# Two transformer blocks with mixtures of experts: the second passes of a pair under one branch behind the down products, the overflow loop moved into the last pair's first unit

## The chip, the cores and the metric

The kernel runs on one core of one Trainium2 chip. The metric is the device time of one execution in microseconds, the median of several runs. Engines: TensorE (PE; PEld is its weight load), VectorE (DVE), ScalarE (ACT), GpSimd (POOL) and SyncE (SP, which issues most loads). A q behind a name (PEq, DVEq, PEldq) is the engine's sequencer, which issues instructions, takes branches and waits on semaphores.

## The reference

Two blocks follow each other on 256 tokens of width 1024: retention and convolution with a mixture of 32 experts, then gMLP and windowed attention with a mixture of 16 experts. Each token goes to two experts. The first mixture, cut to what matters:

```python
eid = grp_idx * EXPERTS_PER_GROUP + top_i
combine = jnp.einsum('nk,nke->ne', top_w, jax.nn.one_hot(eid, N_EXPERTS, dtype=jnp.float32))
y = jnp.zeros(t.shape, jnp.float32)
for e in range(N_EXPERTS):
    h = jax.nn.silu(t @ p['w_exp_gate'][e]) * (t @ p['w_exp_up'][e])
    y = y + combine[:, e:e + 1] * (h @ p['w_exp_down'][e])
```

The second mixture is of the same form with 16 experts. The tokens of one expert are a matter of the data, so the kernel reads counts at run time and branches on them.

## The kernel before

Both mixtures run through `run` (L835). Experts go in pairs: a pair's tokens stand in 64 slots each, gathered by one-hot matmuls into X. Iteration p of the loop does, in this order: the gate and up products of pair p (`unit`, L637, on 32 slots of each expert; `up_more` does the other 32 under a branch, L870, if the expert has more than 32 tokens), with `turn` called between the two halves of the first unit's matmuls; the down products of pair p - 1 (`down`, L676); the gather of pair p + 1 (`gather`, L522, in two PSUM banks); the scatter of pair p - 1 into the sums (`scatter`, L705). Iteration p = n/2 has only the last down products and their scatter. `turn` transposes the hidden rows eh and the one-hots of the pair before (L656, L664) for `down`.

`down` makes two halves o of the output columns, 8 matmul rows each in the built program, with a call `between(o)` in each half after 4 rows. After each half ScalarE makes yh (L679) and VectorE yl (L680).

The first mixture takes at most 64 tokens of an expert this way and the second up to 96: there, `second_up` (branch L787, taken if expert e has more than 64 tokens) does gate and up for 32 more, and `second_down` (L799 for the pair, L802 for each expert) its down products and scatter, two iterations later. Anything beyond goes to `overflow` (L713 to L765; its branch is L719), a loop over a list, one item at a time, which is empty with these data. A count is a register that TensorE, VectorE and ScalarE each load (`count`, L777) before the branch. An engine that skips a body runs a semaphore instruction in its place, so that the counts of the others come out right. With these data only the first expert of pairs 1 and 5 has more than 64 tokens.

Around the change, before: `again(1)`, called in the second half of `down`, holds the second pass of the pair's first expert (`self.second_up(p, 0, ...)`), and the second pass of the other expert stands behind `down`. At the end of iteration np_ - 1 (p = 15 in the first mixture, p = 7 in the second) stands `overflow`. At p = np_ `turn` runs the second downs of the last two pairs under one branch, L854. Experts' weights are loaded by `prefetch` in a fixed order into a ring of slots; the waits of SyncE for a free slot set when a load starts. `x1.work` and `x2.work` name the slot that the overflow loop uses as its scratch.

Of the kernel before, what the change touches and what calls it, by code (L numbers as in the profile page):

```python
# [10 lines left out]
F32 = mybir.dt.float32  # L11
# [46 lines left out]
def block_kernel(ctx: ExitStack, tc: tile.TileContext, a, out, dbg=None):  # L58
# [326 lines left out]
    class Experts:  # L385
# [449 lines left out]
        def run(self, hooks, twice=False):  # L835
            np_ = self.n // 2
# [9 lines left out]
            for p in range(np_ + 1):  # L846
                p1 = p - 1
                ws = prs[p1][2] if p else None

                def turn():  # L850
                    if p == np_ and twice:
                        for e in range(2 * p - 4, 2 * p):
                            self.w(e, 2)
                        with tc.If(self.count(self.n + np_) > 64):  # L854
                            for q in (p - 2, p1):
                                self.second_down(q, more.pop(q))
                    elif p > 1 and twice:
                        self.second_down(p - 2, more.pop(p - 2))
                    if p:
                        hT = turned.pop(1) if 1 in turned else self.turn_h(st.pop(p1))  # L860
                        turned[0] = hT, self.turn_slots(prs[p1][0])
# [11 lines left out]
                def again(o):  # L873
                    if p == np_:
                        return
                    if o == 0:
                        up_more(1)
                    elif twice:
                        more[p] = self.tile("h2", [128, 512], F32, 2)
                        self.second_up(p, 0, more[p], self.gu_bank)  # L880

# [23 lines left out]
                if twice and p < np_:  # L905
                    self.second_up(p, 1, more[p], self.gu_bank)
                if p + 1 < np_:
                    prs[p + 1] = self.pair(p + 1)
                if p:
                    self.scatter(turned[0][1], ys, last=(p1 == np_ - 1))  # L910
                if p == np_ - 1:
                    self.overflow()
                    if not twice:
                        turned[1] = self.turn_h(st.pop(p))
                if p in hooks:
# [735 lines left out]
    x1.slots = [x0, xb, s4, q0, q1, s3, q2, s2, s0, s1]  # L1651
    x1.work = xb
    ident_b = const.tile([128, 128], BF, name="ident_b", tag="colA")
# [399 lines left out]
    x2.slots = x2.slots + [slot_of(ring) for _ in range(3)] + [slot_of(r_) for r_ in ring2]  # L2053
    x2.work = x2.slots[0]
    other = {"PT": "wr32", "P3": "wr16"}
# [74 lines left out]
```

## Time and profile before

| what | value |
|---|---|
| median of 3 runs | 1430.4 us (1430.01 to 1430.69) |
| profiled execution, its own time | 1430.14 us |
| its span in the profile | 1428.3 us |
| granted TensorE clock, mean | 0.967 |
| TensorE busy | 1301.6 us, 91% of the span |
| VectorE, ScalarE, GpSimd busy | 55%, 37%, 19% |
| first mixture | about 548 to 982 us |
| second mixture | about 1165 to 1419 us |

The busy shares are means over stages. In the first mixture the loads of weights run at 427 GB/s in most slices; in the second one the share of the DMA queues is lower in places and TensorE is 88 to 99% busy. The two blocks' other stages are outside the change. The rows below use these names: ms and gu are PSUM banks, w a slot of weights, P one-hots, hb the token rows, rs a row scale, L line numbers of the kernel before.

### The profile page before, as it was taken

What the parts mean: (1) busy time and instruction counts of PE and PEld (TensorE: products, weight loads), DVE (VectorE), ACT (ScalarE), POOL (GpSimd) and SP (SyncE); (2) the same over time, 40 slices, a digit from 0 to 9 for tenths busy, and PEclk for the clock granted to TensorE, in tenths of its full rate; (3) what the DMA queues carried; (4) which work ended last, traced back from release to release, by engine and by line L of the source; (5) the groups of instructions that cost most, each with busy time, mean ns of one, the idle gap of its engine ahead of it and who ended that gap; (6) DMA issues with size and microseconds to landing.
All of it is one profiled execution on the core that took longest, in us unless ns stands there. A gap on an engine that the chain in (4) does not pass through costs nothing. (4 is left out here: it accounts for less than half of the span.)

```text
span 1428.3 us, 25110 instructions
## 1 busy us (share of the span) xinstructions
PE 1301.6 (91%) x10033; PEld 919.4 (64%) x10033; DVE 791.8 (55%) x1555; ACT 528.9 (37%) x889; POOL 273.6 (19%) x308
## 2 busy tenths in 40 slices
PE   7999999999999889978988889998999999889885
PEld 5898999999999784423433334435999964433432
DVE  2898898988965974422423543235664642234222
ACT  1673747455445423221222112224574432222222
POOL 3023424232334310000201300002340410000000
PEclk9999999999999999999999989999999999999998
DMA  9943363554369576999999999997357375999791
GB/s 330 310 158 119 135 227 126 177 185 172 129 185 350 221 293 285 426 427 429 425 429 427 427 427 428 426 398 263 119 223 303 132 293 240 424 415 423 314 404 68
DMA packets 92857, 417.51 MB, mean 292 GB/s; under 512 B 6464, under 2 KB 26832, under 8 KB 75552
## 3 DMA queue, kind: packets, MB, share of 16 engines
q1 hardware_dynamic: 89600, 409.59, 72.5%
q0 software_dynamic: 3104, 5.80, 1.4%
q8 instruction: 106, 1.74, 0.5%
q14 instruction: 47, 0.39, 0.1%
HBM read 414.29 MB, written 1.08 MB: 291 GB/s over the span
## 5 line engine op out<-in xcount | busy, mean ns | idle before, releaser
L676 PE MATMUL ms<-w,hT 128*64 128x512 f32 x768 | 208.4, 643 | 50.8 <-DMA w<-w_exp_down_dram 40.4
L100 DVE TENSOR_TENSOR wlo<-w,whi 128x1024 fp32r<-128x1024 f32 x151 | 196.2, 1301 | 63.5 <-ACT whi L100 63.3
L100 ACT CAST whi<-w 128x1024 fp32r<-128x1024 f32 x158 | 164.8, 1048 | 145.1 <-PE pj L109 139.2
L676 PEld LDWEIGHTS ms<-w,hT 128*64 128x64 f32 x768 | 61.8, 145 | 193.5 <-issue 135.7
L109 PE MATMUL pj<-uh,whi 128*128 128x256 f32 x512 | 148.2, 289 | 0.0
L109 PE MATMUL pj<-ul,whi 128*128 128x256 f32 x512 | 145.8, 285 | 0.9 <-DVE ul L100 0.7
L109 PE MATMUL pj<-uh,wlo 128*128 128x256 f32 x512 | 145.6, 284 | 0.8 <-DVE wlo L100 0.8
L1165 DVE SCALAR_TENSOR_TENSOR cacc<-zT,dwT,cacc 128x256 f32<-128x256 f32 x240 | 141.9, 591 | 3.3
L637 PE MATMUL gu<-w,X 128*32 128x512 f32 x1184 | 140.9, 597 | 1.7 <-DMA w<-w_exp_up_dram 1.4
L645 POOL MEMSET eh<- 32x512 f32 x47 | 24.4, 518 | 545.7 <-DVEq L870 339.9
L109 PEld LDWEIGHTS pj<-uh,whi 128*128 128x128 f32 x512 | 98.7, 193 | 5.0 <-ACT gt L1348 3.4
L109 PEld LDWEIGHTS pj<-ul,whi 128*128 128x128 f32 x512 | 98.7, 193 | 2.0 <-DVE ul L100 1.7
L109 PEld LDWEIGHTS pj<-uh,wlo 128*128 128x128 f32 x512 | 98.7, 193 | 1.0 <-DVE wlo L100 1.0
L637 PE MATMUL gu<-w,h 128*32 128x512 f32 x768 | 92.4, 615 | 2.1 <-DVE eh L643 1.2
L637 PEld LDWEIGHTS gu<-w,X 128*32 128x32 f32 x1184 | 34.0, 109 | 74.6 <-issue 65.8
L657 DVE COPY hT<-ms 128x512 f32<-128x512 f32 x24 | 16.6, 690 | 95.9 <-PE ms L656 95.9
L683 DVE SCALAR_TENSOR_TENSOR yt<-ms,ws,gt 128x512 f32<-128x512 f32 x32 | 24.0, 750 | 81.3 <-PE ms L676 80.1
L100 ACT CAST yh<-yt 128x512 fp32r<-128x512 f32 x32 | 19.8, 620 | 130.6 <-DVE yt L683 130.6
L109 PE MATMUL pj<-hnh,whi 128*128 128x256 f32 x200 | 56.7, 284 | 0.0
L637 PEld LDWEIGHTS gu<-w,h 128*32 128x32 f32 x768 | 24.2, 112 | 50.4 <-issue 45.2
L109 PE MATMUL pj<-hnl,whi 128*128 128x256 f32 x200 | 56.3, 281 | 0.1
L109 PE MATMUL pj<-hnh,wlo 128*128 128x256 f32 x200 | 55.8, 279 | 0.0
(578 smaller groups left out, 2990.6 us busy)
## 6 DMA issues: line engine op xcount, KB each, us to landing
w<-w_exp_gate_dram SPq DMA_DIRECT2D x31, 2048.0 KB, 23.3
w<-w_exp_up_dram SPq DMA_DIRECT2D x31, 2048.0 KB, 26.1
w<-w_exp_down_dram SPq DMA_DIRECT2D x28, 2048.0 KB, 22.3
w<-w_in_dram SPq DMA_DIRECT2D x19, 2048.0 KB, 8.8
w<-expert_w_gate_dram SPq DMA_DIRECT2D x16, 2048.0 KB, 16.5
w<-expert_w_up_dram SPq DMA_DIRECT2D x16, 2048.0 KB, 20.7
w<-w_ada_dram SPq DMA_DIRECT2D x12, 2048.0 KB, 9.4
w<-expert_w_down_dram SPq DMA_DIRECT2D x12, 2048.0 KB, 12.9
```

Of the source, the lines that this page charges most:

```text
L100: return S.copy(hi, src), eng.tensor_sub(lo, src, hi.bitcast(F32))
L109: PE.matmul(out_ap, l(k), r(k), start=(first and i == 0), stop=(last and i == n - 1))
L637: PE.matmul(gu[o:o + 32], x_of(hf * 4 + j), w_of(i, hf * 4 + j), start=(j == 0), stop=(j == 3), tile_position=(0, o))
L645: zero.memset(h[u0 + 32:u0 + 64], 0.0)
L657: V.tensor_copy(hT, p_)
L676: PE.matmul(dn[o][b * 64:b * 64 + 64], hT[:, c, b * 64:b * 64 + 64], w_of(b, c, o), start=(c == 0), stop=(c == 3))
L683: V.scalar_tensor_tensor(y, dn[o], wc, self.gate[:, o * 512:o * 512 + 512], op0=ALU.mult, op1=ALU.mult)
L1165: i = V.scalar_tensor_tensor(cacc[:, j], zT[:, j, w:w + 256], dwT[:, w, j:j + 1], cacc[:, j], op0=ALU.mult, op1=ALU.add)
```

## The change

Both second passes of a pair go under one outer branch (L907 in the changed file), taken if either expert of the pair has more than 64 tokens, behind all of `down`; the inner branches L787 stay inside it. The second down of pair 5 moves from `turn` of p = 7 to the end of p = 6. `overflow` moves from the end of p = np_ - 1 into its `turn`, behind a `prefetch` of all weights. In the first mixture the last pair's hidden rows are transposed ahead of its predecessor's scatter. The overflow scratch becomes another tile in each mixture. Lines behind L851 shift by 3: L854 is L857, L870 is L873.

```diff
--- before.py
+++ after.py
@@ -848,13 +848,16 @@
                 ws = prs[p1][2] if p else None
 
                 def turn():
+                    if p == np_ - 1:
+                        self.prefetch(3 * self.n)
+                        self.overflow()
                     if p == np_ and twice:
                         for e in range(2 * p - 4, 2 * p):
                             self.w(e, 2)
                         with tc.If(self.count(self.n + np_) > 64):
                             for q in (p - 2, p1):
                                 self.second_down(q, more.pop(q))
-                    elif p > 1 and twice:
+                    elif 1 < p < np_ - 1 and twice:
                         self.second_down(p - 2, more.pop(p - 2))
                     if p:
                         hT = turned.pop(1) if 1 in turned else self.turn_h(st.pop(p1))
@@ -875,9 +878,6 @@
                         return
                     if o == 0:
                         up_more(1)
-                    elif twice:
-                        more[p] = self.tile("h2", [128, 512], F32, 2)
-                        self.second_up(p, 0, more[p], self.gu_bank)
 
                 if p < np_:
                     st[p] = self.tile("eh", [128, 512])
@@ -903,15 +903,18 @@
                     again(0)
                     again(1)
                 if twice and p < np_:
-                    self.second_up(p, 1, more[p], self.gu_bank)
+                    more[p] = self.tile("h2", [128, 512], F32, 2)
+                    with tc.If(self.count(self.n + p) > 64):
+                        for b in range(2):
+                            self.second_up(p, b, more[p], self.gu_bank)
                 if p + 1 < np_:
                     prs[p + 1] = self.pair(p + 1)
+                if p == np_ - 1 and not twice:
+                    turned[1] = self.turn_h(st.pop(p))
                 if p:
                     self.scatter(turned[0][1], ys, last=(p1 == np_ - 1))
-                if p == np_ - 1:
-                    self.overflow()
-                    if not twice:
-                        turned[1] = self.turn_h(st.pop(p))
+                if p == np_ - 2 and twice:
+                    self.second_down(p1, more.pop(p1))
                 if p in hooks:
                     hooks[p]()
 
@@ -1649,7 +1652,7 @@
     s0, s1, s2, s3, s4 = [slot_of(r_) for r_ in ring2]
     q0, q1, q2 = [slot_of(ring) for _ in range(3)]
     x1.slots = [x0, xb, s4, q0, q1, s3, q2, s2, s0, s1]
-    x1.work = xb
+    x1.work = lambda: fin["ra"].rearrange("p a n -> p (a n)")
     ident_b = const.tile([128, 128], BF, name="ident_b", tag="colA")
     G.tensor_copy(ident_b, ident)
     halves = h1.bitcast(BF).rearrange("p t (d two) -> p t d two", two=2)
@@ -2051,7 +2054,7 @@
     psp = es.enter_context(pool("pse", 1, space=PSUM))
     x2 = hp["x2"]
     x2.slots = x2.slots + [slot_of(ring) for _ in range(3)] + [slot_of(r_) for r_ in ring2]
-    x2.work = x2.slots[0]
+    x2.work = x2.slots[8]
     other = {"PT": "wr32", "P3": "wr16"}
 
     def tile_of(name, shape, dt=F32, bufs=1):
```

TensorE, from the down products of p = 3 in the second mixture to the gather of pair 4. L676 is down, L777 a count's load, L522 the matmuls of a gather (128x32: those of a second pass, 128x128: those of the next pair). Before:

```order
L676 MATMUL ms<-w,hT 64x512 x8
L777 TENSOR_LOAD over
L787 COMPARE_AND_BRANCH
...
L787 UNCONDITIONAL_BRANCH x2
L676 MATMUL ms<-w,hT 64x512 x4
L777 TENSOR_LOAD over
L787 COMPARE_AND_BRANCH
...
L787 UNCONDITIONAL_BRANCH x2
...
L522 MATMUL ms<-P,hb_11305 128x128
```
Now:

```order
L676 MATMUL ms<-w,hT 64x512 x12
L777 TENSOR_LOAD over
L907 COMPARE_AND_BRANCH
...
L787 COMPARE_AND_BRANCH
...
L787 COMPARE_AND_BRANCH
...
L787 UNCONDITIONAL_BRANCH x2
L907 UNCONDITIONAL_BRANCH
...
L522 MATMUL ms<-P,hb_11305 128x128
```
The branch between 8 and 4 rows of down products is gone; all stand ahead of the branch L907, and both bodies lie in its reach.

VectorE at the same place. L680 makes yl, L538 the one-hots of a second pass, L526 scales the gathered rows. Before:

```order
L680 SCALAR_TENSOR_TENSOR yl<-ms,ws,yh 128x512
L777 TENSOR_LOAD over
L787 COMPARE_AND_BRANCH
L538 TENSOR_TENSOR P_13962<-slot,pos_12367 128x32 x2
...
L787 UNCONDITIONAL_BRANCH x2
L777 TENSOR_LOAD over
L787 COMPARE_AND_BRANCH
...
L787 UNCONDITIONAL_BRANCH x2
L680 SCALAR_TENSOR_TENSOR yl<-ms,ws,yh 128x512
L526 TENSOR_TENSOR h_12373<-ms,cols 128x512
```
Now:

```order
L680 SCALAR_TENSOR_TENSOR yl<-ms,ws,yh 128x512 x2
L777 TENSOR_LOAD over
L907 COMPARE_AND_BRANCH
L777 TENSOR_LOAD over
L787 COMPARE_AND_BRANCH
...
L787 UNCONDITIONAL_BRANCH x2
L777 TENSOR_LOAD over
L787 COMPARE_AND_BRANCH
...
L907 UNCONDITIONAL_BRANCH
L526 TENSOR_TENSOR h_12373<-ms,cols 128x512
```
Both rows of L680 now stand ahead of the branch and of the gather's release; before, the second stood behind both bodies.

TensorE, from the scatter of p = 7 to the last transposes. L705 is the scatter, L718 the load of the overflow count, L656 the transposes of eh. Before:

```order
L705 MATMUL acc_12299<-yl,PT 128x512
L718 TENSOR_LOAD idi
L719 COMPARE_AND_BRANCH
...
L719 UNCONDITIONAL_BRANCH
L777 TENSOR_LOAD over
L854 COMPARE_AND_BRANCH
L777 TENSOR_LOAD over
L799 COMPARE_AND_BRANCH
...
L854 UNCONDITIONAL_BRANCH
L656 MATMUL ms<-ident,eh 128x128 x4
```
Now:

```order
L705 MATMUL acc_12299<-yl,PT 128x512
L777 TENSOR_LOAD over
L857 COMPARE_AND_BRANCH
L777 TENSOR_LOAD over
L799 COMPARE_AND_BRANCH
...
L857 UNCONDITIONAL_BRANCH
L656 MATMUL ms<-ident,eh 128x128 x4
```
The overflow branch is gone from there. It stands in p = 7's first unit now, between two halves of the matmuls of L637 (w are the unit's weights):

```order
L799 UNCONDITIONAL_BRANCH
L637 MATMUL gu<-w,h_12373 32x512 x8
L718 TENSOR_LOAD idi
L719 COMPARE_AND_BRANCH
...
L719 UNCONDITIONAL_BRANCH
L656 MATMUL ms<-ident,eh 128x128 x4
...
L664 MATMUL ms<-ident_b,P 128x128
L637 MATMUL gu<-w,h_12373 32x512 x8
```
Before, the second down of pair 5 stood there in its place; it has moved ahead, to the end of p = 6.

## Rows read from the trace of the kernel before

**Rows 1.** Waits of TensorE, 1160 to 1428 us: total us, times, longest us.
```profile
PE ms L522 <- DVEq L787: 8.8, 3, 4.8
PE ms L656 <- PEq L854: 4.5, 1, 4.5
PE gu L522 <- issue: 4.3, 2, 2.6
PE ms L522 <- PEq L787: 2.6, 1, 2.6
PE ms L656 <- PEq L799: 1.9, 3, 0.7
```

**Rows 2.** Line L787: duration ns min/median/max, first and last start.
```profile
L787 PEldq COMPARE_BRANCH  x18: 70/338/4207, 1176.2 to 1398.0; - x18
```

**Rows 3.** Line L719, the overflow branch, TensorE's sequencer (PEldq) and SyncE's.
```profile
L719 SPq EVENT_SEMAPHORE  x18: 17/17/17, 960.2 to 1394.9; - x18
...
L719 PEldq COMPARE_BRANCH  x2: 428/786/1145, 969.6 to 1401.5; - x2
```

**Rows 4.** Line L854, the branch over the last two second downs.
```profile
L854 PEldq COMPARE_BRANCH  x1: 2457/2457/2457, 1403.3 to 1403.3; - x1
```

**Rows 5.** Timeline of TensorE, p = 2, 3, 4, 6: start, us, what, [idle before <-releaser].
```profile
1238.61 1.94 PE L676 MATMUL ms<-w,hT 128*64 128x512 f32 x8 [1.30 <-PEq L787]
...
1244.19 1.53 PE L522 MATMUL gu<-P,hb 128*128 128x128 bf16 x22 [1.70 <-issue]
...
1273.98 1.68 PE L522 MATMUL ms<-P,hb 128*128 128x128 bf16 x24
...
1279.49 0.41 PE L522 MATMUL gu<-P,hb 128*128 128x128 bf16 x4 [2.60 <-issue]
...
1302.98 1.65 PE L522 MATMUL ms<-P,hb 128*128 128x128 bf16 x24
...
1371.68 1.68 PE L522 MATMUL ms<-P,hb 128*128 128x128 bf16 x24 [2.60 <-PEq L787]
```

**Rows 6.** Timeline of ScalarE, p = 3, the end of the down products.
```profile
1273.87 0.69 ACT L679 ACTIVATE yh<-ms,ws 128x512 fp32r<-128x512 f32 x1 [2.90 <-PE ms L676]
```

**Rows 7.** Timeline of VectorE, p = 3, the same place.
```profile
1274.59 0.75 DVE L680 SCALAR_TENSOR_TENSOR yl<-ms,ws,yh 128x512 fp32r<-128x512 f32 x1 [2.76 <-ACT yh L679]
```

**Rows 8.** Timeline of TensorE, p = 1, with a second pass that runs.
```profile
1203.01 3.06 PE L522 MATMUL gu<-P,hb 128*128 128x32 bf16 x48 [0.54 <-DVE P L538]
...
1206.67 5.34 PE L637 MATMUL gu<-w,h 128*32 128x512 f32 x32 [0.47 <-DVE rs L584]
...
1215.73 1.75 PE L522 MATMUL ms<-P,hb 128*128 128x128 bf16 x24 [1.85 <-DVEq L787]
1217.28 2.76 PE L522 MATMUL gu<-P,hb 128*128 128x128 bf16 x24
```

**Rows 9.** Timeline of VectorE, p = 1.
```profile
1202.69 0.28 DVE L538 TENSOR_TENSOR P<-slot,pos 128x32 bf16<-128x32 f32 x2
...
1214.86 0.47 DVE L793 TENSOR_SCALAR h<-h,rs 32x512 f32<-32x512 f32 x1
```

**Rows 10.** Windows: busy us (x instructions) of PE, PEld, DVE, ACT, POOL; PEclk, DMA share, GB/s.
```profile
1217.20:1220.70 3.50, 3.50 (x32) 3.40 (x31) 0.85 (x2) 0.62 (x3) 0.00 (x0) 0.51 1.03 435
1235.00:1241.00 6.00, 4.55 (x25) 1.56 (x22) 0.75 (x1) 1.11 (x2) 0.00 (x0) 1.00 0.99 415
1406.30:1411.00 4.70, 4.04 (x14) 2.00 (x16) 0.69 (x1) 0.37 (x1) 0.00 (x0) 0.50 0.03 7
```

**Rows 11.** Timeline of TensorE, the last down products.
```profile
1406.34 1.10 PE L656 MATMUL ms<-ident,eh 128*128 128x128 f32 x4 [4.54 <-PEq L854]
...
1408.27 8.83 PE L676 MATMUL ms<-w,hT 128*64 128x512 f32 x32 [0.62 <-ACT PT L665]
```

**Rows 12.** Timeline of TensorE, the last down products of the first mixture.
```profile
971.85 7.09 PE L676 MATMUL ms<-w,hT 128*64 128x512 f32 x32 [0.72 <-ACT PT L665]
```

**Rows 13.** Timeline of GpSimd, the last memset of the second mixture.
```profile
1394.19 0.52 POOL L645 MEMSET eh<- 32x512 f32 x1 [3.02 <-DVEq L870]
```

## Prediction

> **What bounds the kernel now.** I read the waits of TensorE over the second mixture of experts first (iterations p = 0 to 7 and the last down products, from 1160 us on). TensorE waits there for branches and for instructions, never for a weight load: no row of this list names a DMA [rows 1]. In the names, PEq, DVEq and ACTq are an engine's sequencer; "PEq L787" is TensorE's own branch around a second pass, "DVEq L787" VectorE's. "issue" behind the gather L522 is a wait that the profile gives no cause for. So a microsecond taken off these waits comes off the time, and a new one is added to it.
>
> Next, the branch itself [rows 2]. TensorE's jump over a second pass takes 70 to 4207 ns, median 338. The spread tells what it is: a short jump when the code behind it is at hand, and a fetch when it is not. It costs time only if it outlasts the matmuls already queued. The overflow jump takes TensorE 428 and 1145 ns [rows 3], the one over the two last second downs 2457 ns [rows 4].
>
> The timeline shows where it is paid [rows 5]. Second passes run only for the first expert of p = 1 and p = 5; six iterations skip. In p = 2 the first jump, inside the down products, holds TensorE 1.30 us, and the gather behind the second jump stands still 1.70 us in its middle. In p = 3 the stop in the gather is 2.60 us. In p = 4 nothing is paid: the gather starts at once (1302.98). In p = 6 the second jump holds it 2.60 us. Beside these, the start of each gather lies 0.15 us behind the last down product, which is no term.
>
> **The change part by part** (us, after minus before, against the profiled execution's 1430.14; the median of the runs is 0.26 higher). A measurement of this kernel tells about 0.2% from no change, 2.9 us.
>
> *Skipping iterations.* One jump (L907) replaces two. It stands behind all 16 rows of down products, so its fetch can start when they are queued, and the code that it lands on is needed only when they end. Eight matmuls of the profile take 1.94 us [rows 5], and 24 follow the last branch ahead of them: 5.8 us, of which I count 5.3, since the branch's register is loaded first. Before, the second jump had 8 matmuls, 1.94 us, to cover it. The longest jump seen, 4.2 us, fits into 5.3. What is late next is a new wait. The gather's first bank is now released by VectorE's compensation behind L907, and on VectorE the second half of yl (L680) and, before it, yh on ScalarE (L679) now stand ahead of that branch. Before, both stood behind the two branches, so the gather did not wait for them. In p = 3, yh starts at 1273.87, as the last down product ends [rows 6], and yl ends at 1274.59 + 0.75 = 1275.34 [rows 7]. With 0.15 for the signal the gather starts at 1275.5 instead of 1273.98: a gap of 1.65 where 0.15 is. Queued behind L907 on VectorE is only the gather's own scaling (L526), which needs the gather anyway; on ScalarE nothing that is due. Four iterations (2, 3, 4, 6) pay 4 x 1.65 = 6.6. What goes is 1.30 + 0.15 + 1.70, then 0.30 + 2.60, then 0.30, then 0.15 + 2.60: 9.1. I leave 0.7 for a fetch that is still not covered, and get **-1.8**. Bounds: -2.5 if all is covered; +2.5 if half of the old stops stay.
>
> The second passes read gate and up weights until they end or are skipped, so SyncE gets those slots some 2 us later and its loads start later; TensorE waits for no load in this stage [rows 1], so this stays hidden, and would show as a DMA row if it did not.
>
> p = 0 has no down products; its gather waits 4.8 us, the longest row of "DVEq L787" [rows 1], and VectorE's first branch releases it. L907 takes that branch's place: 0. In p = 7 no gather follows: 0.
>
> *Taken iterations, p = 1 and 5.* The second pass's one-hots (L538) ran at 1202.69, while the down products were running, and TensorE waited 0.54 us for them [rows 8, 9]. Now they stand behind yl: 1.5 us after the last down product, as in p = 3, plus 0.28 for the two one-hots and 0.4 for two branches and the signal (what lies between the end of L793, 1215.33, and the gather), 2.2. Entry: +1.66. At its end TensorE waits 1.85 us for L793 and the branch of b = 1 [rows 8, 9], after 8 matmuls of the down products (1.94 us) have run beside that chain. These now come earlier. In their place the first half of the gather runs (1.75 us), which needs only b = 0's early reduction (L584); the second half waits for b = 1's skip, about 1.95. With 0.25 ahead of the first half that is 2.2 against 1.85: +0.35. Together 2 x 2.0 = **+4.0**. [...]
>
> *Overflow jump in p = 7's first unit.* It now stands between the first half of a unit's matmuls and the transposes L656. Nearest rows: the jump over a second down at the same place, 1.9 us in 3 [rows 1], 0.63 each, and the overflow jump itself, up to 1.15 [rows 3]. I take **+1.3** (both costs meet: the jump, and the wait for PE to drain); bounds 0.4 to 3. SyncE's skip waits until all down weights have landed. Before, the loads but one had landed by SyncE's last compensation at 1394.9 [rows 3], and the last 1 MB was held behind it; now it is issued before, and at 415 GB/s [rows 10] lands 2.5 us later, 1397.4. GpSimd's load of the final norm's row and two memsets of 0.52 us [rows 13] queue behind that: done by about 1399.5 (an estimate), and first needed by the last transposes, at 1406.34 before [rows 11] and some 2.5 us earlier now. Hidden; loads that came over 4 us later would be paid one for one. The scratch tile moves to a free slot: 0.
>
> *The end.* TensorE stands still 4.54 us in front of the last transposes [rows 11], for two jumps in a row, 1.15 and 2.46 [rows 3, 4], with their register loads. One of them goes: **-2.5** (bounds -1.2 to -2.9). Behind the stop the clock is granted at 0.50 [rows 10], and the 32 last down products take 8.83 us, where the same 32 take 7.09 at full clock [rows 11, 12]. The stop left is some 2.0 us, below the 2.60 behind which p = 6's gather ran at full clock [rows 5], so I count the whole 1.7 back: **-1.7** (0 to -3.4).
>
> *Second down of pair 5, moved behind p = 6's scatter.* It does the same work, between a unit and a scatter as before: 0. *First mixture.* The overflow jump moves from its end into the last pair's first unit: at its old place it showed 0.4 us [rows 3]; at the new one 0.6 to 1.3. With the transposes now ahead of the scatter I take **+0.9** (-0.8 to +1.5). The next stage's first loads issue behind that jump on SyncE and are due long after: 0.
>
> **Sum:** -1.8 + 4.0 + 1.4 + 1.3 - 4.2 + 0.9 = +1.6 on 1430.14, so about 1431.7; against the median 1432.0. I say **1432.0**.
>
> **Rivals.** *A: the long jump always misses.* One jump now passes two bodies. If both the code it lands on and the code behind that must be fetched, each as long as the longest seen, 4.2 us [rows 2], that is 8.4. Beyond 5.3 of cover and the 1.65 of the new wait 1.45 us shows per skipping iteration: 5.8 for four in place of my 0.7, and 1.45 more at p = 0. The sum is +1.6 + 5.1 + 1.45 = +8.1, 1438.5: slower. It decides once a skip's fetches take over 7 us. For: the stop in p = 3's gather, 2.60 us though its jump was short. Against: p = 4, where two jumps in a row showed nothing [rows 5].
>
> [...]
>
> *B: the clock falls behind the new stops.* Four stops of 1.65 us, each followed by a stretch at the lower level: 4 x 1.1 (the gather's 2.76 against 1.65) is +4.4, so 1436.4. For: the fall behind 1.85 us in p = 1. Against: none behind 2.60 in p = 3 and 6.
>
> *C: the change doesn't bring its wait.* If the gather's bank is released by an instruction ahead of yl, and not by the branch behind it, the 6.6 is 0.6: the sum is -4.4, 1426.0, faster. The order of VectorE's rows speaks against it.
>
> *D: all bounds fall well.* Fetches all covered (-2.5), no clock loss in the taken passes, the overflow jump hidden (+0.4), first mixture -0.8, the end as priced: -2.5 + 4.0 + 0.4 - 4.2 - 0.8 = -3.1, 1427.3.
>
> **How the numbers follow.** My sum 0.66, A 0.12, B 0.08, C 0.07, D 0.07. Around my sum the bounds leave some 3 us either way, so of its 0.66 about 0.03 lies faster than 0.2%, 0.50 within, 0.13 slower. A and B are slower; C and D faster, D half of it within. Faster 0.14, same 0.53, slower 0.33. The range 1427.3 to 1437.5 leaves out C, the far part of A and the edges of my sum, about 0.2.
>
> **What would show it.** In the changed profile: one L907 where two L787 were; a gap of 1.6 us "DVEq L907" before the gathers of p = 2, 3, 4, 6 and no "issue" inside them (stops of over 1 us there: A); 2.2 us before and within the taken second passes; a stop of about 1 us "PEq L719" in p = 7's turn; a stop of 2 us, not 4.5, ahead of the last transposes, and clock 1.0 behind it. I am wrong if the gathers start 0.2 us behind the down products, or if the time lies outside the range.

## The result, and the profile after

The changed kernel takes 1437.8 us (median of 16 runs, 1435.56 to 1448.26) against 1430.84 (16 runs, 1428.74 to 1434.74): ratio 1.0058, 95% interval 1.0045 to 1.0071, so 8.3 us slower (6.4 to 10.2). Forecast were 1.6 us more, 1432.0; the time lies just above the range. The profiled execution took 1443.93 us, a long one among these; the execution behind a second trace of the same kernel (after_again, below) took 1436.51. Both are used.

Where TensorE waits in the second mixture and after it, 1160 to 1442 us, changed kernel (us in total, times, longest), to be read against [rows 1]:

```profile
PE ms L522 <- DVEq L907: 9.8, 4, 4.8
PE gu L522 <- DVE P L538: 4.1, 2, 2.0
PE gu L522 <- DVEq L787: 3.2, 2, 1.6
PE ms L522 <- PEq L907: 2.5, 1, 2.5
PE ms L656 <- issue: 2.4, 1, 2.4
PE gu L637 <- issue: 2.2, 1, 2.2
...
PE acc L705 <- PEq L907: 1.6, 1, 1.6
...
PE ms L656 <- PEq L857: 1.3, 1, 1.3
```

The wait of 4.5 us ahead of the last transposes and the stops inside the gathers are gone from the list. In their place stand the new waits for VectorE's branch and for the late one-hots, which were forecast, and "issue" in two places that were not. Timeline of TensorE in the changed kernel, p = 1, 2, 3 and 6:

```profile
1213.44 3.05 PE L522 MATMUL gu<-P,hb 128*128 128x32 bf16 x48 [2.05 <-DVE P L538]
...
1226.68 1.66 PE L522 MATMUL gu<-P,hb 128*128 128x128 bf16 x24 [1.56 <-DVEq L787]
...
1248.64 1.80 PE L522 MATMUL ms<-P,hb 128*128 128x128 bf16 x24 [1.62 <-DVEq L907]
...
1281.37 1.78 PE L522 MATMUL ms<-P,hb 128*128 128x128 bf16 x24 [1.76 <-DVEq L907]
1282.95 2.77 PE L522 MATMUL gu<-P,hb 128*128 128x128 bf16 x24
...
1378.42 2.75 PE L522 MATMUL ms<-P,hb 128*128 128x128 bf16 x24 [2.52 <-PEq L907]
```

Behind the down products each gather waits 1.62 to 1.76 us (p = 2, 3, 4), 2.52 in p = 6. The second pass's one-hots are waited for 2.05 us, the second half of the gather behind it 1.56. In p = 3 half a gather runs at the lower clock (2.77 us for 24 matmuls; granted 0.50 from 1283.1 to 1285.8 us, where p = 2's gather has 1.00). Now the end of the first mixture, the same view:

```profile
954.59 1.92 PE L637 MATMUL gu<-w,X 128*32 128x512 f32 x16
961.55 1.10 PE L656 MATMUL ms<-ident,eh 128*128 128x128 f32 x4 [5.03 <-PEq L719]
...
962.79 3.20 PE L637 MATMUL gu<-w,X 128*32 128x512 f32 x16
...
967.35 1.94 PE L676 MATMUL ms<-w,hT 128*64 128x512 f32 x8 [1.22 <-PEq L873]
```

Here are 5.03 us that the kernel before doesn't have: TensorE waits for its own sequencer at L719, then runs at the lower clock for a while (3.20 us for 16 matmuls that take 1.92; granted clock 0.61 from 961.5 to 966.5). In the kernel before, the same transposes start without a wait, and the overflow jump, which there stands later, holds the next ones for 0.42 us:

```profile
955.51 0.75 PE L656 MATMUL ms<-ident,eh 128*128 128x128 f32 x4
...
970.30 0.72 PE L656 MATMUL ms<-ident,eh 128*128 128x128 f32 x4 [0.42 <-PEq L719]
```

And p = 7 with the end, changed kernel:

```profile
1393.51 0.72 PE L656 MATMUL ms<-ident,eh 128*128 128x128 f32 x4 [0.48 <-PEq L719]
...
1397.96 1.06 PE L637 MATMUL gu<-w,h 128*32 128x512 f32 x7 [2.21 <-issue]
...
1399.10 5.22 PE L637 MATMUL gu<-w,h 128*32 128x512 f32 x32
...
1413.71 0.71 PE L705 MATMUL acc<-yh,PT 128*128 128x512 f32 x2 [1.60 <-PEq L907]
...
1417.05 0.48 PE L656 MATMUL ms<-ident,eh 128*128 128x128 f32 x2 [1.25 <-PEq L857]
1419.93 0.70 PE L656 MATMUL ms<-ident,eh 128*128 128x128 f32 x2 [2.41 <-issue]
...
1421.46 4.54 PE L676 MATMUL ms<-w,hT 128*64 128x512 f32 x10 [0.62 <-ACT PT L665]
```

The overflow jump itself costs 0.48 us here, but nine matmuls into the next stretch the stream stops for 2.21 us, the next 32 matmuls take 5.22 us where p = 2 and 3 have 3.64 (granted clock 0.75 from 1397.9 to 1404.6 us), and the transposes stop in their middle for 2.41. The branch rows of L719 and L907 (ns min/median/max), against [rows 2, 3]:

```profile
L719 PEldq COMPARE_BRANCH  x2: 452/3334/6217, 955.0 to 1391.6; - x2
```

```profile
L907 PEldq COMPARE_BRANCH  x8: 70/440/6266, 1183.1 to 1408.0; - x8
```

Adding it up over the starts of the gather of p = 0 and of the scatters (us from the span's start; the last columns are the growth within the stretch):

| stretch ends at | before | changed | its second trace | growth | growth, second |
|---|---|---|---|---|---|
| gather, p = 0 | 1180.33 | 1187.26 | 1186.11 | +6.9 | +5.8 |
| scatters of p = 1 and 5 (taken) | | | | +2.0 | +0.1 |
| scatters of p = 2, 3, 4, 6 (skipped) | | | | -0.8 | -2.2 |
| scatter, p = 6 | 1374.73 | 1382.88 | 1378.35 | | |
| scatter, p = 7 | 1399.67 | 1413.71 | 1408.03 | +5.9 | +4.7 |
| last scatter | 1417.03 | 1430.82 | 1423.37 | -0.3 | -2.0 |

The first row holds more than the moved jump. At the scatter of p = 14 in the first mixture, ahead of the moved code, the changed kernel's two traces are already 0.9 and 0.4 us later (952.56 and 952.06 against 951.62). From there to the first mixture's last scatter they take 32.28 and 31.79 us, the kernel before 27.25: +5.0 and +4.5. What is left of the row comes behind that scatter.

### The profile page after: what moved, and what is told of

Same layout as the page of the kernel before. It is cut to its first block, busy times and chain, and to the rows that moved or that the text cites. A ratio compares the mean times of both kernels' runs of the same rounds, so it can differ in the third digit from the quotient of the medians.

```text
span 1442.1 us, 25103 instructions
## 1 busy us (share of the span) xinstructions
PE 1308.6 (91%) x10033; PEld 922.9 (64%) x10033; DVE 792.2 (55%) x1555; ACT 529.5 (37%) x889; POOL 273.0 (19%) x308
## 3 DMA queue, kind: packets, MB, share of 16 engines
q8 instruction: 106, 1.74, 0.5%
## 5 line engine op out<-in xcount | busy, mean ns | idle before, releaser
L676 PE MATMUL ms<-w,hT 128*64 128x512 f32 x768 | 207.3, 644 | 49.4 <-DMA w<-w_exp_down_dram 41.7
L676 PEld LDWEIGHTS ms<-w,hT 128*64 128x64 f32 x768 | 62.4, 146 | 190.6 <-issue 133.8
L637 PE MATMUL gu<-w,X 128*32 128x512 f32 x1184 | 142.5, 601 | 0.4 <-ACT X L531 0.3
L637 PE MATMUL gu<-w,h 128*32 128x512 f32 x768 | 96.4, 633 | 5.2 <-issue 2.2
L637 PEld LDWEIGHTS gu<-w,X 128*32 128x32 f32 x1184 | 35.3, 110 | 73.3 <-issue 63.8
L637 PEld LDWEIGHTS gu<-w,h 128*32 128x32 f32 x768 | 24.5, 115 | 57.0 <-issue 51.4
```

The lines of the kernel that those rows point to most:

```text
L637: PE.matmul(gu[o:o + 32], x_of(hf * 4 + j), w_of(i, hf * 4 + j), start=(j == 0), stop=(j == 3), tile_position=(0, o))
L676: PE.matmul(dn[o][b * 64:b * 64 + 64], hT[:, c, b * 64:b * 64 + 64], w_of(b, c, o), start=(c == 0), stop=(c == 3))
```

## The experiments

Theory 1: the loss is code that TensorE has to fetch. A jump ends in code that is not at hand, or the stream runs into such code soon after, and the fetch is long while weights load. Rivals: the grouping is the loss, by its new waits; or the branches cost their drains (the wait for an engine's own earlier work) and register loads at these places, whatever they skip. VectorE's and ScalarE's branches at L719 take 45 to 63 ns in the changed kernel, so they are not what holds TensorE there. All ratios are to the kernel before, run beside; 0.001 is 1.43 us.

**The two halves apart, and the first trial of code.** *group_only*: the grouped call alone on the kernel before. *overflow_only*: the changed kernel with the old second passes:

```diff
-                    with tc.If(self.count(self.n + p) > 64):
-                        for b in range(2):
-                            self.second_up(p, b, more[p], self.gu_bank)
+                    self.second_up(p, 1, more[p], self.gu_bank)
```

*after_short*, and *before_short* for the kernel before:

```diff
             with tc.If(ni > 0):
-                with tc.For_i(0, ni) as it:
...
+                V.memset(self.work()[:, 0:512], 0.0)
```

*after_short1* and *after_short2* do this in the first or the second mixture alone.

> Only the second passes are grouped (one branch L907-like behind the down products); the overflow branches, the second down of pair 5 and the scratch tiles stay as in the kernel before. Theory 1 (the time went into fetches of code behind the moved overflow jumps): the grouped passes cost what the trace of the changed kernel shows for p = 0 to 6, about +1 us in the taken iterations and -2 to +1 in the skipping ones, so -1 to +3 us against before, and the first mixture ends where it did. Rival (the grouping itself is the loss, by the new wait for yl in each iteration and the clock behind it): +6 us or more.

Measured: 1.0026 (1.0006 to 1.0046), +3.7 us. Above theory 1's -1 to +3 and below the rival's +6, but the interval, 0.9 to 6.6 us, reaches both. The first mixture shows no stop at L719 beyond 0.4 us. At the end, which this run leaves as it was, TensorE stands still for longer than the 4.54 us of [rows 11]:

```profile
PE ms L656 <- PEq L854: 7.3, 1, 7.3
```

> Only the overflow loops move (with the second down of pair 5, the transposes of the first mixture's last pair and the scratch tiles); the second passes stay apart, as before. Theory 1: +5 to +10 us against before, nearly all of the change's loss, with one stop of TensorE of over 3 us behind L719 in the first mixture. Rival (grouping is the loss): -2 to +2 us.

Measured: 1.0024 (1.0008 to 1.0041), +3.4 us, under the 5 to 10 of theory 1; the stop in the first mixture is there, 5.05 us, but the end of the second mixture gave part of it back: from the scatter of p = 7 to the last one it takes 11.59 us, 17.36 before. So neither half is the whole; the two sum to 7.1 of the 8.3.

> The changed kernel with the overflow loop's body replaced by one memset (the handling of listed overflow tokens is left out; the list is empty with these data). The overflow branches, their places, register loads and the drains of the engines stay; only the code that they jump over is gone. Theory 1 (the jump of some 287 instructions of TensorE outruns the code that is at hand): TensorE's L719 takes under 0.7 us in both mixtures, the stop of 5.0 us in the first mixture is under 1, and the time is 7 to 10 us under the changed kernel's, near before's. Rival 2 (the branch costs at its new place whatever it skips, by the drain or by what its registers wait for): no more than 1 us under the changed kernel.

Measured: 0.9988 (0.9977 to 0.9999), -1.7 us, so 10 under the changed kernel: theory 1. The branch and its register are still there, and the transposes start without a wait:

```profile
L719 PEldq COMPARE_BRANCH  x2: 202/212/223, 956.0 to 1389.3; - x2
```

One thing beside the skipped code is gone: TensorE has no work in the short body, so it runs no semaphore instruction at L719 in its place (51 ns each in the changed kernel). That this is not the cause is shown by after_m60 below, which keeps it and waits 0.33 us. With the code gone the new order even gains: from the scatter of p = 14 to the last one the first mixture takes 25.35 us, 27.25 before, 32.28 in the changed kernel.

> The changed kernel with the overflow loop's body replaced by one memset in the first mixture alone (its handling of listed tokens is left out there; the list is empty with these data). Theory 1: the stop of 5.0 us behind L719 in the first mixture and the lower clock behind it go, 5 to 8 us under the changed kernel, 0 to +4 against before; what is left of the loss lies in the second mixture. Rival (it is made up for by later waits for weights of the first mixture, whose loads set its end): within 2 us of the changed kernel.

Measured: 0.9984 (0.9963 to 1.0005), -2.3 us, so 10.6 under the changed kernel: theory 1, and more than the 5 to 8 forecast.

> The changed kernel with the overflow loop's body replaced by one memset in the second mixture alone (its handling of listed tokens is left out there). Theory 1: the first mixture keeps its stop of 5.0 us; in p = 7 the stop inside the first unit (2.2 us) and the clock behind it go: 2 to 5 us under the changed kernel, +3 to +7 against before. Rival (the second mixture's overflow jump costs nothing that other stops don't take over): within 1.5 us of the changed kernel.

Measured: 1.0014 (0.9997 to 1.0031), +2.0 us: 6 under the changed kernel, more than forecast. Its first mixture still stops 4.98 us. Each of the two bodies is worth some 6 us or more, which doesn't add up with the -10 of both; what one gives depends on what the other leaves.

> The kernel before with the overflow loop's body replaced by one memset in both mixtures (the handling of listed tokens is left out; the list is empty with these data). Theory 1: the stop of 4.54 us ahead of the last transposes shrinks to 2 to 3 us, since TensorE then fetches for one jump in place of two; -1 to -4 us against before. Rival (each branch costs its wait whatever it skips): 0 within 1 us.

Measured: 0.9982 (0.9965 to 1.0), -2.6 us, but not at the place: the stop ahead of the last transposes still is 4.12 us in its trace, since the jump of L854 (L815 in that file) now takes 3.1. The sign was right, the reason given was not.

**Real versions.** *after_over1_old* is the changed kernel with the first mixture as before; *overflow2_only* has the second mixture's overflow move alone:

```diff
-                    if p == np_ - 1:
+                    if p == np_ - 1 and twice:
                         self.prefetch(3 * self.n)
                         self.overflow()
...
+                if p == np_ - 1 and not twice:
+                    self.overflow()
+                    turned[1] = self.turn_h(st.pop(p))
```

> The changed kernel with the first mixture's overflow loop (and its scratch and the order of its last transposes) back where it was; the whole computation is done. In the second mixture its instructions stand where the changed kernel's do. Theory 1 (most of the loss is the first mixture's overflow jump): -1 to +3 us against before, 6 to 9 under the changed kernel. Rival (the short body helped for another reason, as by shifting the second mixture's code): +4 us or more against before.

Measured: 1.0023 (1.0004 to 1.0043), +3.3 us, a little over the forecast; 5.9 under the changed kernel beside it. The intervals of the two just overlap. This is the whole computation, and it puts back the scratch and the order of the transposes with the jump; so the first mixture's part of the change is the larger part of the loss.

> The changed kernel once more, for a second trace and times beside the other three. Theory 1: +6 to +10 us against before; in the trace the stop of 5.0 us behind L719 in the first mixture is there again within 0.3 us, since it hangs on where the code stands, while the stops of p = 6 and 7 differ by up to 2 us each.

Measured: 1.0064 (1.0041 to 1.0086), +9.2 us. Its trace shows the first mixture's stop again, and others that are smaller:

```profile
960.99 1.10 PE L656 MATMUL ms<-ident,eh 128*128 128x128 f32 x4 [4.99 <-PEq L719]
```

```profile
1393.59 1.44 PE L637 MATMUL gu<-w,h 128*32 128x512 f32 x7 [2.37 <-issue]
...
1408.03 0.70 PE L705 MATMUL acc<-yh,PT 128*128 128x512 f32 x2 [0.30 <-PEq L907]
...
1413.38 0.51 PE L656 MATMUL ms<-ident,eh 128*128 128x128 f32 x2 [2.14 <-issue]
```

4.99 us against 5.03; in p = 7 the scatter waits 0.30 in place of 1.60.

> The kernel before with the second mixture's overflow loop alone moved into p = 7's first unit (with the second down of pair 5 and its scratch); second passes apart, first mixture as before. Theory 1: the stop ahead of the last transposes, 4.54 us, falls under 1, and p = 7's first unit pays about 1 us: -2 to -6 us against before. Rival (the two places pay the same): within 1.5 us of before.

Measured: 1.0001 (0.9986 to 1.0015): the rival, the two places pay the same. The trace shows how. What the end saves, the first unit of p = 7 pays, with slower matmuls behind it, 16 in 3.64 us where 1.92 is the time of the 16 ahead of the stop:

```profile
1389.80 1.10 PE L656 MATMUL ms<-ident,eh 128*128 128x128 f32 x4 [3.33 <-PEq L719]
...
1391.05 3.64 PE L637 MATMUL gu<-w,h 128*32 128x512 f32 x16
...
1409.81 0.72 PE L656 MATMUL ms<-ident,eh 128*128 128x128 f32 x4 [0.66 <-PEq L857]
...
1411.36 4.08 PE L676 MATMUL ms<-w,hT 128*64 128x512 f32 x18 [0.72 <-ACT PT L665]
```

**The wait for yl.** In the changed kernel yl stands ahead of the branch because each of the two second passes takes a bank for its row scales, and the second bank is the one that yl reads. *group_early* gives both one bank and calls the branch ahead of the second half's yh and yl; *early_over2* does the same to after_over1_old:

```diff
                         with tc.If(self.count(self.n + p) > 64):
+                            held = self.ms([128, 3])
                             for b in range(2):
-                                self.second_up(p, b, more[p], self.gu_bank)
+                                self.second_up(p, b, more[p], self.gu_bank, held)
```

> The kernel before with the second passes grouped under one branch as in the change, overflow as before, and one thing more: both second passes of a pair use one PSUM bank for their row scales, so that the second half's yl stands behind the branch on VectorE again and the next gather does not wait for it. Theory (the new wait is a term of its own, 1.65 us in each of four skipping iterations and 1.5 in each of two taken ones): no wait of 1.6 us for VectorE's branch before the gathers of p = 2, 3, 4, 6; where TensorE's jump lasts over 4 us a stop shows in its place, so not all comes back: 3 to 8 us under the kernel with the grouping alone, so -4 to +1 us against before. Rival (the gathers would have waited for code as long): within 2 us of the grouping alone, +2 to +6 against before.

Measured: 1.0007 (0.9989 to 1.0025), +1.0 us, 2.7 under group_only by these two ratios, whose intervals overlap. The waits are gone, and stops for code are partly in their place:

```profile
1212.85 2.42 PE L522 MATMUL ms<-P,hb 128*128 128x128 bf16 x24 [3.72 <-DVEq L789]
...
1236.38 1.36 PE L522 MATMUL ms<-P,hb 128*128 128x128 bf16 x19 [0.30 <-PEq L902]
1241.50 0.76 PE L522 MATMUL ms<-P,hb 128*128 128x128 bf16 x5 [3.77 <-issue]
```

In p = 2 the gather starts after 0.30 us and then stops for 3.77 in its middle; behind a taken pass it now waits 3.72 for the branch, where the changed kernel's first half ran early.

> The changed kernel with the first mixture's overflow loop back at its old place, and with one PSUM bank for the row scales of both second passes, so that the second half's yl stands behind the branch on VectorE and the gathers don't wait for it. Theory: 2 to 5 us under the kernel with the overflow loop back alone, -5 to -1 against before. Rival (stops for code fill the place of the wait): within 1.5 us of the kernel with the overflow loop back alone.

Measured: 0.9994 (0.9973 to 1.0015), -0.9 us, 4.1 under after_over1_old: as forecast for the difference, though again with overlapping intervals.

**Shifting the code.** Nothing moves here but where the code lies. *after_shift128* and *before_shift128* add 32 narrow matmuls at the start; *over1_m28*, *early_m28*, *before_m28*, *after_m28* take 7 of the 20 warming matmuls there out (28 instructions), *after_m60* takes 15:

```diff
-    keep_warm(idle, 20)
+    keep_warm(idle, 13)
```

> The changed kernel with 32 narrow matmuls added at the very start, in TensorE's wait for the first weights, so that all its later code stands 128 instructions further on. Nothing else moves. Theory 1, as pieces of 16 KB: the jumps fall elsewhere within the pieces, so the stop in the first mixture becomes 1 to 3 us in place of 5.0, and the stops of the second mixture move to other iterations; the time differs from the changed kernel's by over 2 us, either way. Rival 2 (drain or registers): the same stops at the same places, the time within 1 us of the changed kernel's.

Measured: 1.0074 (1.006 to 1.0088).

> The kernel before with 32 narrow matmuls added at the very start, in TensorE's wait for the first weights, so that all its later code stands 128 instructions further on. Theory 1: other jumps pay than in p = 2, 3, 6 and at the end; the sum of TensorE's stops behind branches in the second mixture changes by over 2 us, and the time by as much, either way. Rival (the stops belong to the places): the same stops at the same jumps, the time within 1.5 us of before.

Measured: 1.0021 (1.0005 to 1.0037). These two are inconclusive as times: the added matmuls ran for 9 us, and the first products started at 18.27 us in place of 12.44. As places they fit theory 1: in after_shift128 TensorE waits 0.33 us at L719 in the first mixture in place of 5.03, though 2.73 then behind L873, where it waited 1.22.

> The kernel before with the same 28 instructions less at the start. Theory 1: the stop in p = 2's down products (1.30 us) and those inside the gathers (1.70, 2.60) change place or size, the time moves by 1 to 4 us either way. Rival: the same stops at the same places, within 1 us of before.

Measured: 1.0025 (1.0009 to 1.004), +3.6 us, with the start undisturbed (the first transposes at 20.98 against 21.03). Before, the gather of p = 2 stops after 24 + 2 = 26 matmuls [rows 5: 22 of 48 are left]. The kernel with 28 instructions less:

```profile
1239.79 1.68 PE L522 MATMUL ms<-P,hb 128*128 128x128 bf16 x24
1241.31 1.16 PE L522 MATMUL gu<-P,hb 128*128 128x128 bf16 x16
1245.04 0.66 PE L522 MATMUL gu<-P,hb 128*128 128x128 bf16 x8 [2.58 <-issue]
```

It stops after 24 + 16 = 40: 14 matmuls with their 14 weight loads later, 28 instructions. Two more pairs of runs, which differ by the same 28 instructions, move by the same amount in p = 2's gather: after_over1_old stops after 18 matmuls and over1_m28 after 24 + 8 = 32, early_over2 after 19 and early_m28 after 33. The first of these pairs:

```profile
1250.35 0.76 PE L522 MATMUL ms<-P,hb 128*128 128x128 bf16 x6 [2.23 <-issue]
```

```profile
1247.03 1.18 PE L522 MATMUL gu<-P,hb 128*128 128x128 bf16 x16 [2.14 <-issue]
```

So the stop keeps its place in the code's address, not in the program. This is the plainest evidence. The address says where the next packet of code is needed, not that it comes late: after_m28 stops after 24 + 7 matmuls of the same gather, so by the same 14 the changed kernel needs its packet after 17, and there one ends at 1248.05, before the gather starts, and nothing stops. In before_m28 the stop in p = 2's down products and the one in p = 3's gather are gone, and the one at the end grew from 4.54 to 6.19:

```profile
1410.44 1.10 PE L656 MATMUL ms<-ident,eh 128*128 128x128 f32 x4 [6.19 <-PEq L854]
```

> The changed kernel with 7 of the 20 warming matmuls at the very start left out, so that all later code stands 28 instructions earlier. Counted in the built program and set by the places where TensorE stood still inside a stream of matmuls, the first mixture's overflow branch stands some 5 instructions behind the start of a piece of 256, and its jump of 287 ends in the next piece, whose fetch has only just begun. 28 earlier it stands near the end of the piece ahead, and the jump ends just inside the second piece on, which is not there. Theory 1: the stop of 5.0 us stays or grows, 4.5 to 8 us. Rival (the stop belongs to the place in the program): 5.0 within 0.3 us.

Measured: 1.003 (1.0014 to 1.0045).

> The changed kernel with 15 of the 20 warming matmuls left out: 60 instructions earlier. By the same count the branch then stands some 55 instructions before the end of a piece that was entered long before, and its jump ends in the next piece, which is there. Theory 1: the stop behind L719 in the first mixture is under 1.5 us and its branch under 2.5, the time 3 to 7 us under the changed kernel's, apart from what the second mixture's shifted stops do. Rival: 5.0 within 0.3 us, as in the changed kernel.

Measured: 1.0054 (1.0035 to 1.0073). The first mixture, TensorE, with 28 instructions less:

```profile
957.04 0.72 PE L656 MATMUL ms<-ident,eh 128*128 128x128 f32 x4 [0.33 <-PEq L719]
...
961.57 3.64 PE L637 MATMUL gu<-w,X 128*32 128x512 f32 x16 [3.70 <-issue]
```

and with 60 less:

```profile
958.08 0.72 PE L656 MATMUL ms<-ident,eh 128*128 128x128 f32 x4 [0.33 <-PEq L719]
...
958.84 1.92 PE L637 MATMUL gu<-w,X 128*32 128x512 f32 x16
962.37 0.19 PE L563 MATMUL ms<-wtb,P 128*128 128x6 bf16 x2 [1.60 <-ACT eh L640]
```

With 60 less the stop at the jump is gone (0.33 us, a branch of 330 ns), as theory 1 wants and the rival does not. A smaller one comes behind it, 1.60 us at L563, which ends 1.4 us behind a packet of code like those below (960.98), and the first down products behind it run slowly (8 in 3.33 us, 1.94 in the changed kernel); from scatter to scatter the first mixture takes 29.35 us, between 27.25 before and 32.28. With 28 less I had the size too high: the jump is short, and the stop, 3.70 us, comes in the stream right behind it. With 28 less the time is +4.3 us, with 60 less +7.7: the times don't follow from this one stop. In after_m60 p = 7's jump now stops TensorE for 3.80 us where it was 0.48.

> The changed kernel with the first mixture's overflow loop back at its old place, and with 7 of the 20 warming matmuls at the very start left out (28 instructions), so that the second mixture's code stands 28 instructions earlier. That is, but for one instruction, the place within pieces of 256 instructions that it had with the first mixture's short body. The whole computation is done. Theory 1 (where code stands within its pieces decides which jumps pay): the stops of the second mixture are those of the short body's trace, none over 1 us ahead of the last transposes, one of about 1 us in p = 7's first unit; -5 to 0 us against before. Rival (the short body helped in the first mixture alone): as with the overflow loop back alone, +1 to +6.

Measured: 1.0019 (1.0002 to 1.0035), +2.7 us. The places fit in part (no stop over 1.3 us at the end and none over 0.9 in p = 7's first unit), the gain did not come: the rival.

> The same 28 instructions less at the start, for the kernel with the overflow loop back and the row scales in one bank. The whole computation is done. Theory 1: other stops than without the shift; no forecast of the sign from the places, -6 to +2 us against before. Rival: within 1 us of the unshifted kernel.

Measured: 0.9977 (0.996 to 0.9993), 3.3 us faster than before, with the whole computation. It is the fastest complete version here, and beats both kernels. It was one of several shifts tried, so some of it may be choice. Its end:

```profile
1401.55 0.72 PE L656 MATMUL ms<-ident,eh 128*128 128x128 f32 x4 [1.21 <-PEq L859]
...
1403.10 7.09 PE L676 MATMUL ms<-w,hT 128*64 128x512 f32 x32 [0.72 <-ACT PT L665]
```

**The fetch itself.** The profile names two DMA queues "instruction". One of them, q8, moved 106 packets in the changed kernel, 1.74 MB, 16.4 KB each; that they are TensorE's code is argued from the times that follow. In the kernel before, from 38.5 to 511 us, ahead of the mixtures, 29 of its packets went with 3674 matmuls and 3674 weight loads, 253 instructions to a packet; the pieces of 256 of the expectations are 1% above that. In the stretch of the first mixture's stop, 955.1 to 958.5 us, q8 moves none; in 958.5 to 959.8 one, among 244 packets of weights (queue: packets, MB, share):

```profile
q1 hardware_dynamic: 660, 1.32, 104.4%
```

```profile
q1 hardware_dynamic: 244, 0.48, 100.0%
q8 instruction: 1, 0.02, 5.0%
```

The branch begins at 955.02, the packet starts at 958.67 and ends at 959.72, and the branch ends at 961.24: 3.65 us of waiting for the packet, 1.05 for it, 1.5 behind it. In p = 6 there are 1.4 us from a packet's end to the branch's (1376.73 to 1378.11), and as much inside p = 7's unit (1396.56 to 1397.96). In the twenty traces there are 32 stops of 1.2 us or more from 940 us on that the profile puts down to "issue"; each of them ends 1.3 to 1.6 us behind the end of a packet of q8. That the packet waits because weights fill the queues is argued: the queues moved 387 GB/s in that stretch, and at the end of the kernel before, where they moved 8 GB/s (1399.9 to 1407.5 us), the jump of L854 took 2.46 us in place of 6.2 (at most 4.2 for a jump at that place under 10 GB/s in the other traces); no run emptied the queues at the place of the stop.

## Why the prediction was wrong

By the steps of the sum, with what the two traces of the changed kernel and the runs showed:

- **First mixture, +0.9 (-0.8 to +1.5): the step that failed.** It is +5.0 and +4.5 in the traces, from the scatter of p = 14 to the last one; putting it back takes 5.9 us off (after_over1_old against after_again). The jump stopped TensorE for 5.03 us, and with its code gone the new order is worth -1.9 (after_short). I priced the jump by overflow and second-down rows of 0.4 to 1.3 us. The row with 4.2 us stood in the same table and I used it for the second passes alone. By a count of the built program the jump skips some 287 instructions, with 16 matmuls, 1.9 us, to cover a branch of 6.2. "Its old place showed 0.4" was a property of where its code lay.
- **Overflow jump in p = 7's first unit, +1.3 (0.4 to 3): failed the same way**, +4.7 and +5.9. The jump is as cheap as forecast, 0.43 and 0.48; what was missing is the stop for code behind it (2.2 to 2.4 us), the clock behind that stop (granted 0.75 and 0.73 over the 6.7 and 6.4 us from its end), and in one of the two traces 1.6 us at the scatter. That last wait is L907's in p = 7, which the prediction put at 0 since no gather follows; the scatter waits for it instead (0.30 in the other trace).
- **The end, -4.2: mis-sized**, -0.3 and -2.0. One jump did go, but the code behind the other's target came late, 2.41 and 2.14 us, and the clock fell as before: 32 down products in 9.43 and 8.71 us against 8.83 [rows 11], with 0.75 granted from 1421.4 to 1431 us in the first of these and 0.80 from 1408.2 to 1417.1 before. Where the code lay otherwise the end did gain: -5.8 in overflow_only and -6.0 in overflow2_only, whose p = 7 paid 5.8 for it.
- **Skipping iterations, -1.8: right in these traces**, -0.8 and -2.2. The new wait is 1.62 to 1.76 where 1.65 was forecast, so rival C is out, and the stops in the gathers of p = 2, 3 went. That they went hangs on where the code lies: in group_only's trace the same iterations came to +3.1, with a stop of 2.21 us inside p = 2's gather. The clock fell behind the wait in p = 3 in both traces and in p = 6 in one (in the profiled execution 0.50 and 0.51), not in p = 2 and 4 (1.00), so rival B holds for a part. The cover was not 5.3 us but 4.07 (1242.95, when L907 begins in p = 2, to the last down product's end at 1247.02), so p = 6's fetch of 6.3 us shows 0.9 over the wait.
- **Taken iterations, +5.4: half right.** The stops are as forecast: 2.05 us at the entry (2.2), 0.56 + 1.56 behind it (2.2). But they grew the time by only +2.0 and +0.1: the gather's second half ran at full clock (1.00 from 1226.6 to 1228.4 us, 0.51 before [rows 10]), 1.66 us in place of 2.76, and 24 down products in one piece, 5.37 in place of 3.65 + 1.94. No run shows the 1.4 that the sum has for the clock behind the longer stops; it gave back where I had let it cost (not everywhere: the second pass's own products in p = 5 took 6.56 and 4.93 us in the two traces, 5.34 before).
- **Rival A** (the long jump always misses) holds for p = 6 and p = 7, 6.3 and 5.4 us, and not for p = 0, 2, 3, 0.42 to 0.44, nor for p = 4, whose 1.7 us were covered. I gave it the second passes only; the jumps that mattered were the overflow's. That its 1438.5 lies so near the measured 1437.8 is luck: the iterations that it priced at +3.3 cost -0.8 and -2.2.
- **A misread row.** The 70 ns of [rows 2] are no short jump. They and 73 ns are the branches of p = 1 and 5, whose bodies run; a jump to code at hand took 0.17 to 0.47 us in the changed kernel. The sum doesn't use this number.

Grouping alone came out at +3.7 us (0.9 to 6.6), and the forecast's -1.8 + 4.0 + 1.4 is +3.6. That is luck: in its trace (1441.03 us) the taken iterations are +3.5, but the skipping ones +3.1 and the end +3.5, where -1.8 and nothing were forecast. The second mixture's overflow move alone came out at +0.1 (-2.0 to 2.1), where I had -2.9. What is shown: that the skipped body and the code's address make the stops. Open is why one shift pays in total and another does not: over1_m28 and after_m60 lost most of the stops aimed at, and their times did not follow.

## What to carry to other kernels

A branch around a long body that hardly ever runs is priced by its code (here 6.2 us at L719, and 0.2 with the body replaced by one memset): count the instructions that it skips, and look for work ahead of it that covers a whole fetch under the present load of the queues, here 6.2 us. A branch that was cheap at its old place tells nothing of its new one (0.42 us of waiting here, then 5.03), and neither does a difference of 0.2 to 0.3% between two versions, when 28 instructions at the start of the program can make as much (+3.6 us in before_m28). If two bodies share a branch, look which banks they take: the second one decided here what could stand behind it.

## What was not expected of the hardware

Code lands in packets of 16.4 KB, one at a time (in the traces of both kernels each starts 2.08 us or more behind the end of the one before), and a stream that has run into a missing one goes on 1.3 to 1.6 us after the packet's end (the 32 stops above). Under 423 GB/s of weights (1235.9 to 1249 us) the starts of two packets in a row lie 5.7 and 6.2 us apart (1235.97, 1241.71, 1247.96 in the kernel before), and 3.3 and 3.2 at its end (1400.05, 1403.38, 1406.53), where the weights have landed and 8 GB/s flow. A stop of 1.76 us ahead of p = 3's gather was followed by the lower clock in the middle of it (0.93 from 1281.3 to 1283.1 us, then 0.50), one of 1.62 ahead of p = 2's was not (1.00).
